# A convolution's layer norm emitted behind attention, with the out-projection in two halves

## The chip, the cores and the metric

The kernel runs on one core of one Trainium2 chip. The metric is the device time of one execution in microseconds (us); lower is better. TensorE is called PE here, VectorE DVE, ScalarE ACT, GpSimd POOL; SyncE's queue (SP) issues the DMAs.

## The reference, cut to what matters

Two transformer blocks follow each other on 512 tokens of width 1024. The change touches only the first one. It projects the normalised input, and out of the projection come two branches of 512 channels each: attention with 8 heads over 768 keys, and a convolution branch (a gated input, a depthwise convolution of width 31, a layer norm over the channels, swish, a pointwise product with w_pw). Both are gated, put side by side and multiplied with w_out:

```python
    y = jax.nn.silu(layer_norm(y, ln_w, ln_b))
    return y @ w_pw + b_pw
...
        attn = attend_blocked(q, k_all, v_all) * jax.nn.silu(p[..., ZA_LO:ZA_HI])
        conv = conformer_conv(...) * jax.nn.silu(p[..., ZC_LO:ZC_HI])
        out = jnp.concatenate([attn, conv], axis=-1) @ w_out[l]
        h = h + gate[:, None, :] * out
```

The second block (a recurrent mixer, a memory attention and a feed-forward part) takes h.

## The kernel before, in words

Channels lie on the 128 partitions and the 512 tokens along a row, so that 1024 channels are eight tiles of 128x512. Every large product is made of float32 values split into a high and a low part: `mm3` (line 181) issues three matmuls, high by high, high by low and low by high. A weight tile of 128x1024 is loaded into `wr`, copied by ACT into `wh` (the high part) and subtracted by DVE into `wl` (the rest); `Weights` (line 160) hands the tiles out in the order of its list and loads one ahead. There are two buffers of `wr` and `wl` and three of `wh`.

What is written in the source is an order of emission. A planner puts each engine's instructions into one fixed order by it: an instruction emitted earlier has priority, and one that could start sooner by the planner's own estimates may overtake it. On the chip each engine works through its order and waits where an operand is late. Two rules bind the planner further. The first writes of the buffers of one name come in the order in which the buffers were asked for (`wrote`, line 71). And `k.after` (line 84) puts an instruction behind another one that is named.

In the stretch of interest, from some 160 to 347 us, the first block does this:

- The convolution (`conv`, line 488) is 120 multiply-adds on DVE, written `hg<-hg,c` in the trace. They are emitted with a priority 1500 lower, so that they fill DVE's holes.
- Attention runs in eight half-steps, two for each pair of heads: `scores` (line 720) makes products into the PSUM tile `s` (two buffers of two banks), their maximum on DVE and the exponential into `p` on ACT; `values` (line 740) turns `p` around by PE transposes into `pt`, copies them by ACT into `xb`, and multiplies with the values into `pv`, in six chunks. The values of a half-step are emitted behind the scores of the next one. After both halves of a pair `att_out` (line 752) spreads the reciprocal sums through a buffer `tA` and four transposes, and multiplies; `att_split` (line 763) splits the result into `cat[0]` to `cat[3]`.
- `ln_pw` (line 662) is a generator that goes on by one step with each `next`: (1) the mean over channels by four matmuls with a constant matrix into `pj`, put behind the last matmul of attention emitted so far (`mark[0]`), and four subtractions; (2) four squares into `tA` and their sum; (3) the variance by small matmuls, a square root and a reciprocal; (4, 5) the reciprocal spread by transposes, and for each of four tiles the norm, the swish and the split, through `tA`; (6 to 9) the four pointwise products into `pj`, each with its gate and split into `cat[4]` to `cat[7]`. `LN_AFTER` (line 334) says behind which half-step each step is emitted: the mean behind the scores of half-step 4, steps 4 and 5 behind 5.5 and 6.5, the last three products behind 7.5.
- The out-projection (line 803) makes eight tiles of eight blocks each, the convolution's four blocks first, and takes a PSUM tile in turn from `pj`, `pt`, `pt` and `pv`. Each tile gets its gate and the input added (`xa`), is stored to `h1d`, and is split and squared for the next norm.

The first block has all eight PSUM banks: `pj` one, `s` two buffers of two, `pt` two, `pv` one.

Of the kernel before, what the change touches and what calls it, by code (L numbers as in the profile page):

```python
# [22 lines left out]
P = 128  # L23
S = 512
# [115 lines left out]
def split(k, src, hi, lo, dep=None):  # L140
    r = k.A.activation(hi, src, AF.Copy)
    if dep is not None:
        k.after(r, dep)
    rest(k, src, hi, lo)
# [15 lines left out]
class Weights:  # L160
# [14 lines left out]
    def next(self):  # L175
        i = self.i = getattr(self, "i", -1) + 1
        self.fill(i + 1 + self.ahead)
        return self.got[i]


def mm3(k, ps, wh, wl, ah, al, first, last):
    mm = k.T.matmul
    mm(ps, wh, ah, start=first, stop=False)
    mm(ps, wh, al, start=False, stop=False)
    k.mm = mm(ps, wl, ah, start=False, stop=last)
    return k.mm


def proj(k, ps, w, acts, order=None, tick=None):
    wh, wl = w  # L190
    order = list(order or range(len(acts)))
    for i, kt in enumerate(order):
        c = slice(kt * P, (kt + 1) * P)
        r = mm3(k, ps, wh[:, c], wl[:, c], acts[kt][0], acts[kt][1], i == 0, i == len(order) - 1)
        if tick:
            tick(r, 3)
# [67 lines left out]
def bcast(k, r, n, tag):  # L264
    b = k.t(tag)
    for j in range(n):
        k.T.transpose(b[:, j * P:(j + 1) * P], r[:, j:j + 1].to_broadcast([P, P]), k.ident)
    return b
# [62 lines left out]
    k.hka = small(k, k.vec("k_a", 0, 6), 6, 0.5)  # L331
    k.oka = small(k, k.vec("k_a", 0, 6), 6, -0.5, 1.0)

LN_AFTER = (4, 4.5, 5, 5.5, 6.5, 7, 7.5, 7.5, 7.5, 8)
MODW = 10
LATER = 1500
CTX = (0, 2)
# [3 lines left out]
def block1(k, I, st, h1d):  # L341
# [88 lines left out]
    ps = k.t("pj")  # L430
# [28 lines left out]
    for j in range(KT):  # L459
        raw, wh, wl = raws[j], k.t("wh", [1024], F32R), k.t("wl", [1024], F32R)  # L460
# [12 lines left out]
        for m in range(6):  # L473
            c = slice(m * P, (m + 1) * P)
# [13 lines left out]
    def conv(i):  # L488
# [3 lines left out]
        with k.tc.high_priority(offset=-LATER):  # L492
            for w in range(31):
                if w != 15:
# [2 lines left out]
                                           op0=ALU.mult, op1=ALU.add)  # L497

    W1 = Weights(k, [I["w_in"][0], I["w_in"][1]] + [I["w_q"][g] for g in range(4)] + [I["w_kv"][g] for g in range(2)]
                 + [I["w_in"][i] for i in (6, 7, 8, 9, 2, 3, 4, 5)] + [I["w_pw"][i] for i in range(2)] + [I["w_out"][i] for i in range(8)])  # L500
    W1.fill(1)
    for i in range(3):
        glu(accs[2 * i], accs[2 * i + 1])
# [13 lines left out]
    for g in range(4):  # L517
        wh, wl = W1.next()
        for kk in range(2):
            j = 2 * g + kk  # L520
            c = slice(kk * S, (kk + 1) * S)
            for t in range(4):
                tt = slice(t * P, (t + 1) * P)
                uh, ul = us[j]
                ps = q_ps[t // 2][:, t % 2, :]
# [18 lines left out]
    for t in (2, 3, 4, 5, 0, 1):  # L544
        ps = k.t("pt", [256])
        for j in range(KT):
            wh, wl = kw[j // 4]
            c = slice((j % 4) * 256, (j % 4 + 1) * 256)
            uh, ul = cus[j] if t < 2 else us[j]
            o = (t if t < 2 else t - 2) * P  # L550
# [76 lines left out]
    def zgates(n):  # L627
        for _ in range(min(n, 8 - len(gz))):
            i = len(gz)
            gz.append(zgate(zt[i] if i < 4 else "pj"))  # L630
# [19 lines left out]
    for g in range(2):  # L650
        for o, ts_ in ((0, range(2, 6)), (512, range(0, 2))):
            b = k.t("pt")
            n = len(ts_) * P
# [7 lines left out]
    cat = [None] * KT  # L661
    def ln_pw():
        mean = k.t("pj")
        for i in range(4):
            k.after(T.matmul(mean, k.ones512, ys[i], start=i == 0, stop=i == 3), mark[0])
        for i in range(4):
            V.tensor_tensor(out=ys[i], in0=ys[i], in1=mean, op=ALU.subtract)
        yield
        ss = SumSq(k, "tA")
        for i in range(4):  # L670
            ss.add(ys[i])
        yield
        r = ss.rstd("pj", k.inv512, 1e-6, k.cal([4]))
        yield
        rb = bcast(k, r, 4, "pj")
        ysl = []
        for i in range(4):
            V.tensor_tensor(out=ys[i], in0=ys[i], in1=rb, op=ALU.mult)
            t = k.t("tA")
            A.activation(t, ys[i], AF.Tanh, bias=k.hlb[:, i:i + 1], scale=k.hlw[:, i:i + 1])  # L680
            A.activation(ys[i], ys[i], AF.Identity, bias=k.vec("conv_ln_b", i), scale=k.vec("conv_ln_w", i))
            V.scalar_tensor_tensor(out=t, in0=t, scalar=1.0, in1=ys[i], op0=ALU.add, op1=ALU.mult)
            yh, yl = k.t("U", dt=F32R), k.t("U", dt=F32R)
            split(k, t, yh, yl)
            ysl.append((yh, yl))
            if i % 2:
                yield
        for m in range(4):
            if m % 2 == 0:
                wh, wl = W1.next()  # L690
            ps = k.t("pj")
            for j in range(4):
                c = slice((m % 2) * 512 + j * P, (m % 2) * 512 + (j + 1) * P)
                mm3(k, ps, wh[:, c], wl[:, c], ysl[j][0], ysl[j][1], j == 0, j == 3)
            t = k.t("tA")
            V.scalar_tensor_tensor(out=t, in0=ps, scalar=k.bpw2[:, m:m + 1], in1=gzc[m], op0=ALU.add, op1=ALU.mult)
            ch, cl = k.t("U", dt=F32R), k.t("U", dt=F32R)
            A.activation(ch, t, AF.Copy, scale=0.25)
            V.scalar_tensor_tensor(out=cl, in0=t, scalar=0.25, in1=ch.bitcast(F32), op0=ALU.mult, op1=ALU.subtract)
            cat[4 + m] = (ch, cl)  # L700
            k.dump("cat", 4 + m, ch.bitcast(F32))
            yield
# [4 lines left out]
    order = [2, 3, 4, 5, 0, 1]  # L707
    def heads(pr):
        qs = []
        for hh in range(2):  # L710
            h = 2 * pr + hh
            b = k.t("pt")
            for t in range(4):
                T.transpose(b[:, t * P:(t + 1) * P], flat(qr[t][pr // 2][:, h % 4]), k.ident)
            qhi, qlo = k.t("xa", dt=F32R), k.t("xa", dt=F32R)
            split(k, b, qhi, qlo)
            qs.append((qhi, qlo))
        return qs
# [21 lines left out]
    def values(pr, half, pts, pv):  # L740
        g = pr // 2
        for c in range(6):
            b = k.t("pt")
            for i in range(4):
                T.transpose(b[:, i * P:(i + 1) * P], pts[i][:, c * P:(c + 1) * P], k.ident)
            pT = k.t("xb")
            A.activation(pT, b, AF.Copy)
            for hh in range(2):
                mark[0] = T.matmul(pv[hh * 64:(hh + 1) * 64, half * 256:(half + 1) * 256], kvs[order[c]][:, 128 + g * 64:192 + g * 64],
                                   pT[:, hh * 256:(hh + 1) * 256], start=c == 0, stop=c == 5)  # L750
# [12 lines left out]
    def att_split(pr):  # L763
        ch, cl = k.t("U", dt=F32R), k.t("U", dt=F32R)
        split(k, gz[4 + pr], ch, cl)
        cat[pr] = (ch, cl)

    ln = ln_pw()
    zgates(ZG[1])
    qs = heads(0)  # L770
    zgates(ZG[2])
    pend, done = None, []
    for pr in range(4):
        for half in range(2):
            i = 2 * pr + half
            pts = scores(pr, half, qs)
            zgates(ZG[3 + i])
            for _ in range(LN_AFTER.count(i)):
                next(ln, None)
            if half == 1 and pr < 3:  # L780
                qs = heads(pr + 1)
            if len(gz) == 8:
                while done:
                    att_split(done.pop(0))
            if pend is not None:
                if pend[1] == 0:
                    pv = k.t("pv")
                values(*pend, pv)
                if pend[1] == 1:
                    att_out(pend[0], pv)  # L790
                    done.append(pend[0])
            for _ in range(LN_AFTER.count(i + 0.5)):
                next(ln, None)
            pend = (pr, half, pts)
    values(*pend, pv)
    att_out(3, pv)
    att_split(3)
    for _ in ln:
        pass

    S2.close()
    nm = Norm(k, "norm_mix_g", "hg", "xb")
    for m in range(KT):
        ps = k.t(("pj", "pt", "pt", "pv")[m % 4])
        proj(k, ps, W1.next(), cat, order=[4, 5, 6, 7, 0, 1, 2, 3])
        h = k.t("xa")
        Y.dma_start(out=h, in_=I["xT"][:, m, :])
        V.scalar_tensor_tensor(out=h, in0=ps, scalar=gate[:, m:m + 1], in1=h, op0=ALU.mult, op1=ALU.add)
        Y.dma_start(out=h1d[m], in_=h)
        k.dump("h1", m, h)  # L810
        nm.add(m, h)
# [677 lines left out]
def f32(a):  # L1489
    return np.ascontiguousarray(np.asarray(a), dtype=np.float32)  # L1490


def stat(w, cols):
    w = f32(w)
    kt = w.shape[0] // P
    return np.stack([w[:, c:c + P].reshape(kt, P, P).transpose(1, 0, 2).reshape(P, kt * P) for c in cols])
# [9 lines left out]
def pairs(w):  # L1506
    return np.ascontiguousarray(w.reshape(w.shape[0] // 2, 2, P, w.shape[2]).transpose(0, 2, 1, 3).reshape(w.shape[0] // 2, P, 2 * w.shape[2]))
# [7 lines left out]
def prepare(x, c, ctx, c_ctx, w_mod, b_mod, norm_w, w_in, q_norm_w, k_norm_w, conv_w, conv_b, conv_ln_w, conv_ln_b,  # L1515
# [3 lines left out]
    I = {}  # L1519
# [6 lines left out]
    w = f32(w_in[0])  # L1526
# [3 lines left out]
    I["w_q"] = mov(w[:, 0:512], 2)  # L1530
    I["w_kv"] = mov(w[:, 512:768], 4)
    I["w_pw"] = pairs(stat(w_pw[0], [128 * i for i in range(4)]))
    I["w_out"] = stat(w_out[0], [128 * i for i in range(8)])
    sw = np.concatenate([np.arange(16, 32), np.arange(0, 16), np.arange(48, 64), np.arange(32, 48)])
    qn, kn = f32(q_norm_w[0]), f32(k_norm_w[0])
    I["rows"] = f32(np.stack([qn, qn[sw], kn, kn[sw], f32(mem_q_norm_g_2[0]), f32(mem_k_norm_g_2[0])]))
# [46 lines left out]
```

## Time and profile before

| | us |
|---|---|
| median of 3 runs | 1144.32 |
| lowest and highest | 1142.23, 1146.53 |
| the profiled execution | 1144.24 |
| its span, first to last instruction | 1142.5 |
| PE busy in the span | 1084.6 (95%) |
| DVE, ACT busy | 726.8, 537.5 |
| PE's mean granted clock, as a share of 2.4 GHz | 0.979 |

The span is the time that the rows count from. A row of a timeline gives its start, its duration, the engine, the instruction with what it writes and reads, how many such instructions are merged in it, and in brackets how long the engine was idle before it and who released it. PE's rows overlap at their ends, since matmuls are pipelined; the distance from start to start is what one costs in a stream. All instructions pass through a helper and bear the same line number, L57, so they are told apart by their tiles.

### The profile page before, as it was taken

To read this page: it belongs to the slowest core of one execution; us is meant where nothing else is said; L and a number is where in the kernel's file an instruction comes from. 1 tells how busy PE (TensorE), PEld (TensorE's weight loads), DVE (VectorE), ACT (ScalarE), POOL (GpSimd) and SP (SyncE) were. 2 spreads that over 40 slices of the span, in tenths; PEclk is the share of its full clock that TensorE was granted. 3 is DMA by queue.
4 is the path that set the end of the run, shared out by engine and by line. 5 is a ranking of instruction groups with operands and counts; after the bars stand their busy time and mean duration, and the time that the engine had idled before them with its cause. 6 is when DMAs were issued, how large, how long until landed. Compare 5 with 4: busy or idle time off the path is not lost.

```text
span 1142.5 us, 15940 instructions
## 1 busy us (share of the span) xinstructions
PE 1084.6 (95%) x6272; PEld 836.6 (73%) x6272; DVE 726.8 (64%) x1253; ACT 537.5 (47%) x987; POOL 67.6 (6%) x223
## 2 busy tenths in 40 slices
PE   8989989985998899999999898999999999999998
PEld 3768966553787677777777676768888888888887
DVE  3469999986354688888876888657444334334332
ACT  5344546767335366464645565555434134233220
POOL 0000000000001112111111112010000000000000
PEclk8999999997999999999989998999999999999999
DMA  9653221000243111010101221212222333233232
GB/s 337 258 182 105 73 76 38 1 30 26 71 151 118 55 46 49 20 38 20 38 20 52 74 75 38 74 56 93 92 93 93 95 107 93 92 95 107 93 116 88
DMA packets 32203, 96.46 MB, mean 84 GB/s; under 512 B 3456, under 2 KB 6272, under 8 KB 32128
## 3 DMA queue, kind: packets, MB, share of 16 engines
q1 hardware_dynamic: 32128, 95.45, 25.3%
q8 instruction: 49, 0.80, 0.3%
q14 instruction: 26, 0.21, 0.1%
HBM read 91.24 MB, written 4.19 MB: 84 GB/s over the span
## 4 chain that ended last, share of the span: by engine, by line
PE 83%; DVE 5%; ACT 4%; POOL 3%; DMA 2%; issue 2%; SPq 0%; ACTq 0%; POOLq 0%; DVEq 0%
PE pf L57 31%; PE pj L57 23%; PE pt L57 7%; PE i L57 7%; PE s L57 7%; PE pv L57 5%; PE y L57 3%; POOL nr L57 3%; DVE hg L57 1%; ACT p L57 1%; ACT tA L57 1%; DVE c L57 1%; ACT wh L57 1%; DMA x<-xT 1%; DMA wr<-rw_in 1%
## 5 line engine op out<-in xcount | busy, mean ns | idle before, releaser
L57 ACT ACTIVATE wh<-wr 128x1024 fp32r<-128x1024 f32 (+1 forms) x132 | 137.6, 1043 | 186.7 <-PE pf L57 74.6
L57 DVE TENSOR_TENSOR wl<-wr,wh 128x1024 fp32r<-128x1024 f32 (+1 forms) x132 | 158.7, 1203 | 20.3 <-PE pt L57 12.6
L57 PE MATMUL pf<-A,wh 128*128 128x512 f32 x512 | 157.8, 390 | 0.0
L57 PE MATMUL pj<-hg,wh 128*128 128x512 f32 x448 | 153.6, 415 | 2.5 <-ACT r L57 1.1
L57 ACT ACTIVATE f<-i 128x512 f16<-128x512 f32 (+1 forms) x132 | 71.9, 598 | 91.5 <-PE i L57 91.4
L57 PEld LDWEIGHTS pf<-A,wh 128*128 128x128 f32 x512 | 96.0, 188 | 19.8
L57 PE MATMUL pf<-A,wl 128*128 128x512 f32 x256 | 99.7, 389 | 0.0
L57 PEld LDWEIGHTS pj<-hg,wh 128*128 128x128 f32 x448 | 80.7, 191 | 19.6 <-issue 2.0
L57 DVE TENSOR_TENSOR x<-x,pf 128x512 f32<-128x512 f32 (+1 forms) x33 | 22.2, 672 | 113.9 <-PE pf L57 113.9
L57 PE MATMUL pj<-hg,wl 128*128 128x512 f32 x224 | 90.4, 404 | 1.5 <-DVE wl L57 1.5
L57 DVE SCALAR_TENSOR_TENSOR hg<-hg,c 128x499 f32<-128x499 f32 (+14 forms) x120 | 85.0, 739 | 0.8 <-ACT hg L57 0.4
L57 PE MATMUL pf<-ff,wh 128*128 128x512 f32 (+1 forms) x272 | 79.7, 377 | 0.0
L57 PE MATMUL pf<-hg,wh 128*128 128x512 f32 x256 | 78.8, 389 | 0.0
L57 DVE SCALAR_TENSOR_TENSOR fr<-pf,r 128x512 f32<-128x512 f32 x32 | 22.1, 691 | 85.4 <-PE pf L57 82.1
L57 ACT ACTIVATE fr<-fr 128x512 f32<-128x512 f32 x32 | 20.2, 632 | 99.9 <-DVE fr L57 99.9
L57 PEld LDWEIGHTS <-f 128*128 128x128 f16 x720 | 45.8, 100 | 23.0 <-issue 13.3
L57 PE MATMUL i<-f 128*128 128x128 f16 x672 | 55.6, 225 | 5.4 <-DVE f L57 5.3
L57 PE MATMUL pj<-U,wh 128*128 128x512 f32 x160 | 54.2, 416 | 3.4 <-DVE hg L57 3.0
L57 PEld LDWEIGHTS pf<-ff,wh 128*128 128x128 f32 x272 | 50.1, 188 | 9.5
L57 PEld LDWEIGHTS pf<-A,wl 128*128 128x128 f32 x256 | 48.1, 188 | 10.0
L57 PEld LDWEIGHTS pf<-hg,wh 128*128 128x128 f32 x256 | 48.1, 188 | 10.0
L57 PE MATMUL pf<-ff,wl 128*128 128x512 f32 (+1 forms) x136 | 51.2, 377 | 0.0
(305 smaller groups left out, 2125.8 us busy)
## 6 DMA issues: line engine op xcount, KB each, us to landing
wr<-w_ff SPq DMA_DIRECT2D x64, 512.0 KB, 3.5
modw<-w_mod SPq DMA_DIRECT2D x20, 512.0 KB, 7.2
wr<-rw_in SPq DMA_DIRECT2D x20, 512.0 KB, 3.5
wr<-w_out SPq DMA_DIRECT2D x16, 512.0 KB, 3.5
wr<-w_in SPq DMA_DIRECT2D x10, 512.0 KB, 3.6
wr<-w_start SPq DMA_DIRECT2D x8, 384.0 KB, 5.8
x<-xT SPq DMA_DIRECT2D x8, 256.0 KB, 6.1
modw<-w_mod SPq DMA_DIRECT2D x8, 256.0 KB, 6.2
```

Source lines behind the costliest of these rows:

```text
L57: r = f(*a, **kw)
```

## The change

`LN_AFTER` goes, and with it the steps of `ln_pw` between the half-steps. When all of attention is emitted, five steps of `ln_pw` follow (up to the norm's split), then the out-projection's attention half for the tiles 0 to 5, then the pointwise products, then the attention half of the tiles 6 and 7, then the convolution's half of all eight tiles. The eight sums stay open in the eight PSUM banks meanwhile: four in the two `s` buffers, two in `pt`, one each in `pj` and `pv`. The tiles 0 to 3 take the first three blocks of attention first and the fourth behind them. The pointwise products take `pj` and `pv` in turn. The weights of the out-projection are stored in two halves, two tiles to a load; there are as many loads of the same size as before, in another order.

```diff
--- before.py
+++ after.py
@@ -331,7 +331,6 @@
     k.hka = small(k, k.vec("k_a", 0, 6), 6, 0.5)
     k.oka = small(k, k.vec("k_a", 0, 6), 6, -0.5, 1.0)
 
-LN_AFTER = (4, 4.5, 5, 5.5, 6.5, 7, 7.5, 7.5, 7.5, 8)
 MODW = 10
 LATER = 1500
 CTX = (0, 2)
@@ -497,7 +496,8 @@
                                            op0=ALU.mult, op1=ALU.add)
 
     W1 = Weights(k, [I["w_in"][0], I["w_in"][1]] + [I["w_q"][g] for g in range(4)] + [I["w_kv"][g] for g in range(2)]
-                 + [I["w_in"][i] for i in (6, 7, 8, 9, 2, 3, 4, 5)] + [I["w_pw"][i] for i in range(2)] + [I["w_out"][i] for i in range(8)])
+                 + [I["w_in"][i] for i in (6, 7, 8, 9, 2, 3, 4, 5)] + [I["w_outa"][i] for i in range(3)]
+                 + [I["w_pw"][i] for i in range(2)] + [I["w_outa"][3]] + [I["w_outb"][i] for i in range(4)])
     W1.fill(1)
     for i in range(3):
         glu(accs[2 * i], accs[2 * i + 1])
@@ -688,7 +688,7 @@
         for m in range(4):
             if m % 2 == 0:
                 wh, wl = W1.next()
-            ps = k.t("pj")
+            ps = k.t(("pj", "pv")[m % 2])
             for j in range(4):
                 c = slice((m % 2) * 512 + j * P, (m % 2) * 512 + (j + 1) * P)
                 mm3(k, ps, wh[:, c], wl[:, c], ysl[j][0], ysl[j][1], j == 0, j == 3)
@@ -775,8 +775,6 @@
             i = 2 * pr + half
             pts = scores(pr, half, qs)
             zgates(ZG[3 + i])
-            for _ in range(LN_AFTER.count(i)):
-                next(ln, None)
             if half == 1 and pr < 3:
                 qs = heads(pr + 1)
             if len(gz) == 8:
@@ -789,20 +787,47 @@
                 if pend[1] == 1:
                     att_out(pend[0], pv)
                     done.append(pend[0])
-            for _ in range(LN_AFTER.count(i + 0.5)):
-                next(ln, None)
             pend = (pr, half, pts)
+    oacc = []
+
+    def outa(m, w, kts):
+        wh, wl = w
+        for kt in kts:
+            c = slice(m % 2 * 512 + kt * P, m % 2 * 512 + (kt + 1) * P)
+            mm3(k, oacc[m], wh[:, c], wl[:, c], cat[kt][0], cat[kt][1], kt == 0, False)
+
     values(*pend, pv)
     att_out(3, pv)
     att_split(3)
+    for _ in range(5):
+        next(ln)
+    w01 = [W1.next(), W1.next()]
+    for i in range(2):
+        a = k.t("s", [2, S])
+        oacc += [a[:, 0, :], a[:, 1, :]]
+    for kts in ((0, 1, 2), (3,)):
+        for m in range(4):
+            outa(m, w01[m // 2], kts)
+    w = W1.next()
+    for m in (4, 5):
+        oacc.append(k.t("pt"))
+        outa(m, w, range(4))
     for _ in ln:
         pass
+    w = W1.next()
+    for m in (6, 7):
+        oacc.append(k.t(("pj", "pv")[m % 2]))
+        outa(m, w, range(4))
 
     S2.close()
     nm = Norm(k, "norm_mix_g", "hg", "xb")
     for m in range(KT):
-        ps = k.t(("pj", "pt", "pt", "pv")[m % 4])
-        proj(k, ps, W1.next(), cat, order=[4, 5, 6, 7, 0, 1, 2, 3])
+        if m % 2 == 0:
+            wh, wl = W1.next()
+        ps = oacc[m]
+        for kt in range(4):
+            c = slice(m % 2 * 512 + kt * P, m % 2 * 512 + (kt + 1) * P)
+            mm3(k, ps, wh[:, c], wl[:, c], cat[4 + kt][0], cat[4 + kt][1], False, kt == 3)
         h = k.t("xa")
         Y.dma_start(out=h, in_=I["xT"][:, m, :])
         V.scalar_tensor_tensor(out=h, in0=ps, scalar=gate[:, m:m + 1], in1=h, op0=ALU.mult, op1=ALU.add)
@@ -1530,7 +1555,8 @@
     I["w_q"] = mov(w[:, 0:512], 2)
     I["w_kv"] = mov(w[:, 512:768], 4)
     I["w_pw"] = pairs(stat(w_pw[0], [128 * i for i in range(4)]))
-    I["w_out"] = stat(w_out[0], [128 * i for i in range(8)])
+    for n, o in (("w_outa", 0), ("w_outb", 512)):
+        I[n] = pairs(stat(f32(w_out[0])[o:o + 512], [128 * i for i in range(8)]))
     sw = np.concatenate([np.arange(16, 32), np.arange(0, 16), np.arange(48, 64), np.arange(32, 48)])
     qn, kn = f32(q_norm_w[0]), f32(k_norm_w[0])
     I["rows"] = f32(np.stack([qn, qn[sw], kn, kn[sw], f32(mem_q_norm_g_2[0]), f32(mem_k_norm_g_2[0])]))
```

## Rows read from the trace of the kernel before

**Rows 1.** Windows, by stage: length, busy us of each engine, PEclk, DMA share, GB/s.

```profile
160.00:254.20 94.20, 87.40 (x529) 59.69 (x528) 85.68 (x146) 61.92 (x120) 0.00 (x0) 1.00 0.07 23
254.20:274.70 20.50, 7.51 (x31) 5.35 (x30) 14.25 (x27) 13.80 (x22) 0.00 (x0) 0.72 0.17 52
274.70:304.30 29.60, 29.15 (x155) 18.20 (x154) 13.63 (x20) 15.86 (x27) 0.00 (x0) 0.96 0.12 36
304.30:347.00 42.70, 42.70 (x190) 35.31 (x188) 22.66 (x30) 16.07 (x22) 0.00 (x0) 1.00 0.38 130
```

**Rows 2.** Windows of 2 us, one inside the gap, same columns.

```profile
264.00:266.00 2.00, 1.19 (x6) 1.19 (x6) 0.81 (x2) 1.70 (x3) 0.00 (x0) 0.50 0.01 4
```

**Rows 3.** Timeline of PE, 254 to 277: start, us, instruction, idle before and releaser.

```profile
254.20 0.74 PE L57 MATMUL s<-kst,xa 128*128 128x512 f32 x3
255.89 0.97 PE L57 MATMUL s<-kst,xa 128*128 128x512 f32 x4 [0.95 <-ACT p L57]
257.88 0.98 PE L57 MATMUL s<-kst,xa 128*128 128x512 f32 x4 [1.02 <-ACT p L57]
258.92 1.12 PE L57 MATMUL pj<-hg,c 128*128 128x512 f32 x2
264.81 1.86 PE L57 MATMUL pj<-g,tA 128*128 128x1 f32 x8 [4.77 <-DVE tA L57]
267.25 1.11 PE L57 MATMUL pj<-g,c 128*128 128x128 f32 x4 [0.57 <-DVE c L57]
273.98 1.11 PE L57 MATMUL pt<-g,tA 128*128 128x128 f32 x4 [5.62 <-ACT tA L57]
274.74 1.28 PE L57 MATMUL pj<-U,wh 128*128 128x512 f32 x2
```

**Rows 4.** Timeline of ACT and DVE in the same stretch.

```profile
273.31 0.61 ACT L57 ACTIVATE tA<-c 128x512 f32<-128x512 f32 x1
258.14 0.72 DVE L57 SCALAR_TENSOR_TENSOR hg<-hg,c 128x497 f32<-128x497 f32 x1
279.48 0.69 DVE L57 TENSOR_TENSOR U<-tA,U 128x512 fp32r<-128x512 f32 x1 [0.22 <-ACT U L57]
```

**Rows 5.** Timeline of PE, one stretch of attention values and of the first mean.

```profile
212.28 1.18 PE L57 MATMUL pv<-xb,kvs 128*64 128x256 f32 x8
213.39 1.10 PE L57 MATMUL pt<-g,p 128*128 128x128 f32 x8
214.25 0.94 PE L57 MATMUL s<-kst,xa 128*128 128x512 f32 x4
223.62 2.74 PE L57 MATMUL pj<-hg,c 128*128 128x512 f32 x6
```

**Rows 6.** Timeline of PE at the next block's start.

```profile
341.32 0.62 PE L57 MATMUL pv<-U,wh 128*128 128x512 f32 x2
346.76 0.61 PE L57 MATMUL pj<-hg,wh 128*128 128x512 f32 x2
348.90 0.50 PE L57 MATMUL pj<-hg,wl 128*128 128x512 f32 x1 [1.52 <-DVE wl L57]
354.06 0.95 PE L57 MATMUL pj<-g,xb 128*128 128x1 f32 x8
355.57 0.65 PE L57 MATMUL pj<-g 128*128 128x128 f32 x4 [0.57 <-DVE g L57]
```

**Rows 7.** Timeline of ACT and DVE, the first out-projection weights.

```profile
289.93 1.06 ACT L57 ACTIVATE wh<-wr 128x1024 fp32r<-128x1024 f32 x1 [2.24 <-PE pj L57]
290.84 1.22 DVE L57 TENSOR_TENSOR wl<-wr,wh 128x1024 fp32r<-128x1024 f32 x1
```

**Rows 8.** Timeline of PE at its lower clock.

```profile
157.08 1.03 PE L57 MATMUL pj<-U,wh 128*128 128x512 f32 x2 [2.50 <-DVE hg L57]
158.33 1.05 PE L57 MATMUL pj<-U,wh 128*128 128x512 f32 x2
```

**Rows 9.** SyncE's queue, the load of the seventh tile's input.

```profile
311.75 0.33 SPq L57 DMA_DIRECT2D xa<-xT  x1
```

## The prediction

> **What bounds the kernel now.** I read the stages first. Over the span PE is busy 95%, so only a stage in which PE waits can give much back. From 160 to 254 us PE is busy 87.4 of 94.2 us and DVE 85.7: attention and convolution together keep both near full. From 304 to 347 us, the out-projection, PE is busy all of 42.7 us. Between them PE does 7.5 us of work in 20.5 us, at a mean clock of 0.72 [rows 1], and inside it the clock stands at 0.50, the lower level of 1.2 GHz [rows 2].
>
> PE's timeline says what these 20 us are. After the last scores and the mean it waits 4.77 us for DVE's sum of squares, 0.57 for the reciprocal, and 5.62 for ACT's buffer `tA` [rows 3]. The last wait matters most. What PE waits for is `att_out` of the third pair, four transposes that need no more than attention's sums. Their input is written at 273.31, after the norm's tanh [rows 4], because both use `tA` and the norm asked for it first. The values of the last two half-steps ask for `pt` behind those transposes, so twelve chunks of ready attention work stand behind the layer norm. The norm in turn waits for the convolution, whose last multiply-add starts at 258.14 [rows 4]. So the stage is bound by one chain, convolution, norm, swish, during which PE has work that it may not touch.
>
> **The work of the stretch.** I take it from the start of the last scores, 254.20 [rows 3], to the first matmul of the next block, 346.76 [rows 6]: 92.6 us. PE's work in it, at full clock:
> - scores: 0.74 + 0.97 + 0.98 = 2.7 us [rows 3].
> - values, twelve chunks: two chunks take 1.97 us from start to start (212.28 to 214.25 [rows 5]), so six times that, 11.8 us.
> - two `att_out`: four transposes cost 0.65 at full clock in the next block's norm [rows 6], so 1.3 us.
> - the mean: eight records; six took 2.74 [rows 5], so 3.7 us. Before, only two of the eight stood inside the stretch (1.12 us [rows 3]), so 2.6 us of them are new there.
> - variance and spread, 0.95 + 0.65 = 1.6 us [rows 6].
> - pointwise product and out-projection: 48 + 192 matmuls. A tile of 24 takes 5.44 us (341.32 to 346.76 [rows 6]), 0.227 each, together 54.4 us. Halving the out-projection's tiles leaves the count of matmuls as it is.
>
> Sum 75.5 us. The slack of before is 17.1 us: waits 0.95 + 1.02 + 4.77 + 0.57 + 5.62 = 12.9 [rows 3]; the lower clock, 0.9 for the variance, 0.5 for each of two groups of transposes (against [rows 6]) and about 1 for the first pointwise matmuls, 2.9; and 1.3 left over at changes between kinds of matmuls, which I keep.
>
> **What the change removes and adds.**
> - *Order of buffers.* Attention asks for `tA` and `pt` ahead of the norm now. The values of half-step 6 can follow those of 5 at 254 us, beside the scores. This takes away the 5.62 us wait. What is late next is the exponential of the last scores: PE idles 7% from 160 to 254 [rows 1], and 7% of the 17 us of attention work left is 1.2 us. Bounds 0 (tiles of the out-projection fill it) and 3.
> - *An added wait.* The mean stands behind the last values matmul, hence near 272 instead of 259, and ends near 275. Behind it in PE's order stand up to six half tiles, 6 x 2.72 = 16.3 us, which need only `cat[0]` to `cat[3]`. From the mean's end to the first pointwise matmul took 14.7 us (260.04 to 274.74 [rows 3]), to the fourth split pair 20.1 (280.17 [rows 4]). With the variance and the spread at full clock that is 18.7. Cover: 16.3 + 1.6, and the first pointwise tile's three blocks 2.0, 19.9 in all. So the chain is just hidden. But tiles that the planner sets ahead of the mean don't cover it. I expect some 3 us ahead, hence 2.0 us of idleness. Bounds: 0 with none ahead; 7 with the first 36 matmuls (8.2 us) ahead.
> - *Weights.* The third load's split waits until the first weights are free, after tile 1's fourth block. ACT and DVE need 2.1 us (289.93 to 292.06 [rows 7]) against 1.36 us of matmuls of tiles 2 and 3. Its `wl` stands in DVE's queue among the norm's steps, and they behind it. I take 0.5 us, bounds 0 and 2.5. The later loads have 5.4 us of matmuls each, as before.
> - *The second half's cover.* `cat[4]` to `cat[7]` have the attention half of tiles 6 and 7 over them, 5.4 us; gate and split take some 2.1 (three steps of about 0.7, as [rows 4]). Nothing, up to 1 if buffers of `U` come late.
> - *The tail.* A tile leaves every 2.72 us instead of 5.44. DVE was busy 22.7 us for about eight tiles [rows 1], 2.8 each, so it is level with PE at the end. The next block already waited 1.52 us for DVE's `wl` [rows 6]. I take 0, bounds -1.5 and +1.5. SP issues as many loads and stores as before, in half the time; the stage moved 130 GB/s, and the second half would move about double in its 22 us. The seventh input is asked for when the first tile has left, at 311.75, 7.5 us into the stage [rows 1, 9]; that would do in the second half too, where it is needed after 16 us. PE waits for no evacuation, since all eight sums have their own bank.
>
> Left idle: 1.3 + 1.2 + 2.0 + 0.5 = 5.0. Gain 17.1 - 5.0 = 12.1 us. The profiled execution took 1144.24 us, 0.08 below the median of 1144.32, so both give 1132.
>
> **The rivals.**
> - *All covered* (0.11). No idleness beyond the 1.3 us, and the next block loses its 1.52 us wait: 17.1 - 1.3 + 1.5 = 17.3 us, 1127. For it: 19.9 us of cover against 18.7. Against: PE's fixed order, in which any misjudged step costs.
> - *Half covered* (0.12). The first 36 matmuls stand ahead of the mean: 7.0 us idle under the chain, about 3 us of lower clock as before, and 1 us for the weights. Gain 17.1 - 1.3 - 11.0 = 4.8, 1139.5. For it: the four `s` sums come free with the last exponentials, well before the mean.
> - *Slower: the chain stands bare at another place* (0.06). All six half tiles run ahead of the mean. Then 18.7 - 1.6 - 2.0 = 15.1 us idle and 2.9 of lower clock stand against a slack of 17.1 - 1.3 = 15.8: 2.2 us lost, with the weights' 0.8 and the tail's 1.5 some 4.5, 1149. It decides from about 13 us of tiles ahead of the mean on. Against it: filling needs holes in PE, and attention's tail has only a few us of them.
> - *Clock* (0.03). Moving from sum to sum in six banks with short waits keeps PE at 1.2 GHz through the attention half. Three matmuls took 1.25 us there (157.08 to 158.33 [rows 8]) instead of 0.68: 24 x 0.57 = 13.7 us, 1146. The Trainium skill, "TensorE: Matmul & The Clock Gate", section "A second HAM failure mode: psum-queue depth-cycling", tells of a kernel that lost its full clock again and again in the small waits while it cycled through PSUM banks. By that rule the forecast would fall to this rival; the trace speaks against it, since before the out-projection changed banks every 24 matmuls at clock 1.00 [rows 1].
> - *Nothing moves* (0.04). Another shared buffer ties attention's tail to the norm as `tA` did: 1144. I found none: `s`, `p`, `xb` and `pv` are asked for by attention first.
>
> **How the numbers follow.** The forecast has 0.64. A measurement of this kernel can tell about 0.5%, 5.7 us. Forecast, the first rival and half of the second lie beyond it: 0.81 faster. The other half, clock, nothing-moves and the milder part of the slower rival: 0.13 the same. Slower by more: 0.06. The range holds the forecast with its bounds, most of the first rival and of the second: 1126.5 to 1139.5.
>
> **What would show it.** Right: transposes of `p` follow at 254 without the 5.62 us wait; the mean comes near 272 with eight records in a row; `pt<-U` matmuls stand between it and the pointwise ones; PEclk 1.00 throughout; the next block starts near 334.5. Wrong: waits of PE for `tA` or `c` over 4 us in all after the mean, a clock of 0.50 there, tiles of the out-projection ahead of the mean by more than 8 us, or a longer wait for `wl` at the next block's start.

## The result, and the profile after

The changed kernel took 1128.38 us (median of 4 runs, 1126.26 to 1130.51) against 1143.74 for the kernel before, run beside it (4 runs, 1142.23 to 1146.53). The ratio is 0.9875 with a 95% interval of 0.9851 to 0.9898: 14.3 us less, between 11.7 and 17.0. The two medians lie 15.4 us apart; the 14.3 is worked out from the ratio. The forecast was 1132.0 and a gain of 12.1.

The profiled execution took 1126.26 us (span 1124.5) against 1144.24 (span 1142.5). Of these 18.0 us, 3.5 are not the change's: both programs give PE the same instructions up to 223 us, yet the first pair's `att_out` already stands at 205.64 before

```profile
205.64 0.60 PE L57 MATMUL pt<-g,tA 128*128 128x128 f32 x4
```

and at 202.16 after:

```profile
202.16 0.60 PE L57 MATMUL pt<-g,tA 128*128 128x128 f32 x4
```

Runs of one and the same program differ nearly as much: three of the kernel called "first weights" below have it at 202.47, 205.80 and 204.35. The granted clock of the first 40 us is 0.87 before and 1.00 after, but that is not all of it, since the three have 1.00, 0.91 and 1.00 there. From here on I measure from that `att_out`, which takes the difference out.

The profile's first part after the change, PE's line: busy time, share of the span, instructions.

```profile
PE 1076.2 (96%) x6272; PEld 832.4 (74%) x6272; DVE 726.4 (65%) x1253; ACT 537.6 (48%) x987; POOL 67.5 (6%) x223
```

The changed kernel by stage, the columns as in [rows 1]. The stages are bounded by the second and third pair's `att_out`, the mean, the first pointwise matmul, the end of the out-projection, and the next block's first matmul on `lw`.

```profile
223.68:246.40 22.72, 20.92 (x143) 14.14 (x142) 20.76 (x36) 16.64 (x32) 0.00 (x0) 1.00 0.07 24
246.40:266.33 19.93, 19.12 (x133) 12.51 (x132) 10.78 (x20) 12.04 (x23) 0.00 (x0) 1.00 0.17 54
266.33:286.80 20.47, 19.53 (x85) 14.48 (x84) 14.41 (x22) 12.75 (x18) 0.00 (x0) 1.00 0.17 51
286.80:326.17 39.37, 38.90 (x169) 31.00 (x167) 27.02 (x36) 18.47 (x27) 0.00 (x0) 1.00 0.41 134
326.17:359.04 32.87, 27.66 (x117) 22.25 (x117) 14.80 (x20) 15.35 (x21) 5.66 (x11) 0.90 0.37 118
```

The stage that was 37% busy at a clock of 0.72 [rows 1] is gone. From 246.40 to 326.17 PE does nothing for 0.81 + 0.94 + 0.47 = 2.2 us, at a clock of 1.00 throughout. The last line is the exception, at 0.90 with 5.2 us in which PE is idle; the same stretch before is shorter, at 1.00 with 3.2 us idle:

```profile
346.92:374.75 27.83, 24.63 (x117) 20.03 (x116) 13.31 (x18) 12.64 (x17) 5.18 (x11) 1.00 0.40 130
```

PE's timeline after the change (start, us, instruction, idle before and releaser), against [rows 3]:

```profile
246.40 0.60 PE L57 MATMUL pt<-g,tA 128*128 128x128 f32 x4
...
256.03 0.71 PE L57 MATMUL s<-U,wh 128*128 128x512 f32 x2
...
264.77 1.14 PE L57 MATMUL pv<-xb,kvs 128*64 128x256 f32 x8
...
266.33 3.60 PE L57 MATMUL pj<-hg,c 128*128 128x512 f32 x8
...
274.81 0.95 PE L57 MATMUL pj<-g,tA 128*128 128x1 f32 x8
...
277.78 0.60 PE L57 MATMUL pj<-g,c 128*128 128x128 f32 x4
...
282.09 0.50 PE L57 MATMUL pt<-U,wl 128*128 128x512 f32 x1 [0.94 <-DVE wl L57]
...
286.80 0.61 PE L57 MATMUL pj<-U,wh 128*128 128x512 f32 x2
...
293.06 0.74 PE L57 MATMUL pj<-U,wh 128*128 128x512 f32 x2 [0.47 <-DVE tA L57]
```

The third `att_out` comes without a wait. Nine matmuls of the out-projection (`s<-U`, from 256.03) fill holes of attention's tail; then the mean stands as eight records in a row. Half tiles lie around the variance (274.81) and the spread (277.78), so neither shows the waits of 4.77 and 0.57 that it had. The view of PE's waits from 246 to 327 (us in total, times, longest) is all that is left:

```profile
PE pt L57 <- DVE wl L57: 0.9, 1, 0.9
PE pv L57 <- ACT xb L57: 0.7, 2, 0.3
PE pj L57 <- DVE tA L57: 0.5, 1, 0.5
```

So against before, in the profiled pair: 2.6 us less up to the second `att_out` (24.08 to 21.52 from the first one), 14.7 less from there to the end of the out-projection, 5.0 more at the next block's start (27.83 to 32.87), and 2.3 less in the 765 us behind it. Together 14.5. The last term can't be put down to the change: among all kernels below, whose program is the same there, this distance went from 763.8 to 768.7 us.

### The profile page after: what moved, and what is told of

Its sections match the earlier page's. It is cut to its first block, busy times and chain, and to the rows that moved or that the text cites. A ratio compares the mean times of both kernels' runs of the same rounds, so it can differ in the third digit from the quotient of the medians.

```text
span 1124.5 us, 15949 instructions
## 1 busy us (share of the span) xinstructions
PE 1076.2 (96%) x6272; PEld 832.4 (74%) x6272; DVE 726.4 (65%) x1253; ACT 537.6 (48%) x987; POOL 67.5 (6%) x223
## 4 chain that ended last, share of the span: by engine, by line
PE 83%; DVE 5%; ACT 4%; POOL 3%; DMA 3%; issue 2%; SPq 0%; ACTq 0%; DVEq 0%; POOLq 0%
PE pf L57 31%; PE pj L57 22%; PE s L57 9%; PE i L57 7%; PE pt L57 6%; PE pv L57 5%; PE y L57 3%; POOL nr L57 3%; DMA modw<-w_mod 1%; ACT p L57 1%; DMA wr<-w_start 1%; DVE wl L57 1%; DVE hg L57 1%; ACT wh L57 1%; ACT xb L57 1%
## 5 line engine op out<-in xcount | busy, mean ns | idle before, releaser
L57 PEld LDWEIGHTS <-f 128*128 128x128 f16 x720 | 46.0, 100 | 23.7 <-issue 14.7
L57 PEld LDWEIGHTS pj<-hg,wl 128*128 128x128 f32 x224 | 42.9, 192 | 9.8 <-DVE wl L57 1.3
```

The lines of the kernel that those rows point to most:

```text
L57: r = f(*a, **kw)
```

## The experiments

"Stretch" is from the first `att_out` to the end of the out-projection, "entry" from there to the first matmul on `lw`, both of the profiled execution; the median is of all runs of a kernel. Each ratio is against runs of the kernel before made beside it, whose median went from 1142.50 to 1143.82, so differences to the first line's median do not give it.

| kernel | stretch, us | entry, us | median, us | ratio (95%) |
|---|---|---|---|---|
| before | 141.28 | 27.83 | 1143.74 | |
| changed | 124.01 | 32.87 | 1128.38 | 0.9875 (0.9851 to 0.9898) |
| own buffer | 136.87 | 30.21 | 1141.06 | 0.9983 (0.9959 to 1.0006) |
| whole tiles | 140.08 | 28.13 | 1142.48 | 1.0011 (0.9985 to 1.0038) |
| old place | 138.07 | 31.19 | 1143.10 | 0.9990 (0.9967 to 1.0013) |
| two tiles | 134.35 | 33.10 | 1139.60 | 0.9976 (0.9952 to 1.0000) |
| four tiles | 129.63 | 31.91 | 1134.61 | 0.9930 (0.9903 to 0.9957) |
| block order | 124.65 | 30.50 | 1128.58 | 0.9871 (0.9849 to 0.9894) |
| first weights | 124.03 | 29.89 | 1127.37 | 0.9862 (0.9833 to 0.9891) |
| first weights in before | 141.24 | 28.02 | 1143.53 | 1.0006 (0.9981 to 1.0030) |
| changed, again | 124.07 | 33.11 | 1128.84 | 0.9877 (0.9847 to 0.9907) |
| first weights, again | 124.08 | 26.93 | 1124.18 | 0.9844 (0.9816 to 0.9872) |
| changed, third | 124.01 | 31.34 | 1128.94 | 0.9862 (0.9838 to 0.9886) |
| first weights, third | 124.00 | 27.20 | 1127.01 | 0.9852 (0.9827 to 0.9877) |

### Own buffer: the tie through `tA` cut, nothing else

```diff
 (before)
-    k.open(S2, "att", dict(q2=8, p=8))
+    k.open(S2, "att", dict(q2=8, p=8, rx=1))
...
-        rx = k.t("tA", [8, 64])
+        rx = k.t("rx", [8, 64])
```

> The kernel before with one edit: the spread sums of att_out get a buffer of their own (rx) instead of one of the norm's tA. Theory 'tie' (the gap is attention standing behind the norm through tA): the values of the last two half-steps move into the gap, the 5.62 us wait of the transposes goes, and the norm's chain (14.7 us to the first pointwise matmul, 20 to the fourth pair) runs beside 15.8 us of attention work; some 5 to 8 us of idleness stay. 1144 - 10 = 1134 us, between 1131 and 1137. Theory 'cover' (only the six half tiles of the out-projection can fill the chain): attention alone changes little, 1140 to 1144 us.

The stretch became 4.4 us shorter. The median is 1.4 us below the 1142.50 of the kernel before beside it, and the ratio's interval holds 1: the tie by itself is not the 12 us. PE's timeline of this kernel:

```profile
276.65 0.50 PE L57 MATMUL pj<-U,wh 128*128 128x512 f32 x1 [4.27 <-ACT U L57]
...
282.92 0.50 PE L57 MATMUL pj<-U,wh 128*128 128x512 f32 x1 [0.96 <-DVE U L57]
...
284.58 0.73 PE L57 MATMUL pj<-U,wh 128*128 128x512 f32 x2 [0.93 <-DVE tA L57]
...
288.44 0.74 PE L57 MATMUL pj<-U,wh 128*128 128x512 f32 x2 [0.84 <-DVE tA L57]
...
292.35 0.74 PE L57 MATMUL pj<-U,wh 128*128 128x512 f32 x2 [0.39 <-DVE tA L57]
...
296.25 0.74 PE L57 MATMUL pj<-U,wh 128*128 128x512 f32 x2 [0.84 <-DVE tA L57]
```

The 5.62 us wait is gone, and the freed values now run under the variance's wait of 4.77. But they are used up before the swish, on which PE waits 4.27; and where they had stood between the pointwise products, those now wait for their one sum's bank to be read out, 0.93 + 0.84 + 0.39 + 0.84 = 3.0 us. These waits, with one of 0.23 behind the first, are 8.5 us, and five of 0.23 to 0.31 for `xb` are 1.4 more; they stand in place of the 12.9 [rows 3]. Over the stretch PE's idle time falls from 17.2 to 13.5 us and its busy time, at a clock of 0.99 instead of 0.95, from 124.1 to 123.3, which makes the 4.4. The ready work that the tie held back had been covering something later.

### Whole tiles: the norm behind attention, nothing to cover it

```diff
 (changed)
-    for _ in range(5):
-        next(ln)
...
     for _ in ln:
         pass
...
-        ps = oacc[m]
...
+        ps = k.t(("pj", "pt", "pt", "pv")[m % 4])
+        proj(k, ps, W1.next(), cat, order=[4, 5, 6, 7, 0, 1, 2, 3])
```

The out-projection and its loads are whole again, as before; the pointwise products still take `pj` and `pv` in turn.

> The changed kernel without its halves: the whole norm and the pointwise product behind attention, then the out-projection whole in eight tiles of 24 matmuls. Theory 'cover': attention is untied but the chain lies bare, some 15 us of idleness and 3 us of lower clock more than in the changed kernel: 1128.4 + 17 = 1145 us, 1142 to 1148. Theory 'tie': untying is what pays, 1131 to 1137 us.

The same time as before, the stretch 1.2 us shorter. PE's timeline has the whole chain bare, 4.76 + 0.57 + 6.33 us, and the doubled 1.86, 1.11 and 1.52 us of the lower clock behind each wait:

```profile
275.02 1.86 PE L57 MATMUL pj<-g,tA 128*128 128x1 f32 x8 [4.76 <-DVE tA L57]
277.45 1.11 PE L57 MATMUL pj<-g,c 128*128 128x128 f32 x4 [0.57 <-DVE c L57]
284.89 1.52 PE L57 MATMUL pj<-U,wh 128*128 128x512 f32 x2 [6.33 <-ACT U L57]
```

### Old place: the half tiles, with the norm's steps inside attention

```diff
 (changed)
+LN_AFTER = (4, 4.5, 5, 5.5, 6.5)
...
+            for _ in range(LN_AFTER.count(i)):
+                next(ln)
...
-    for _ in range(5):
-        next(ln)
```

> The changed kernel with the norm's first five steps emitted between the half-steps again, at the old places 4, 4.5, 5, 5.5 and 6.5; the halves of the out-projection stay, six half tiles ahead of the pointwise product. Theory 'tie': att_out of the third pair stands behind the norm's tA again, so the gap of 259 to 274 us comes back and the six tiles, which need attention, come too late to fill it: 1140 to 1145 us. Theory 'cover': the six tiles are there to fill the chain wherever it stands: 1127 to 1132 us.

The stretch is 3.2 us shorter, and the entry 3.4 us longer. The half tiles that PE can reach take the place of the norm's early waits (4.77 and 0.57 are gone, 2.64 for `p` stands there), but the others come behind `att_out` of the third pair, which has its wait for `tA` back to the hundredth, 5.62 us, with the lower clock's 1.12 behind it.

```profile
262.77 0.73 PE L57 MATMUL s<-U,wh 128*128 128x512 f32 x2 [2.64 <-ACT p L57]
...
271.36 1.12 PE L57 MATMUL pt<-g,tA 128*128 128x128 f32 x4 [5.62 <-ACT tA L57]
```

So untying alone gives 4.4 us of the stretch, the late norm without cover 1.2, cover without untying 3.2; the change, which has all, 17.3.

### Two tiles and four tiles: the dose

```diff
 (changed)
-    for m in (4, 5):
...
     for _ in ln:
         pass
+    for m in (4, 5):
...
```

The diff is that of the four tiles, without the order of the loads, which follows it; the two-tile kernel moves half tiles 2 and 3 behind as well.

> The changed kernel with two half tiles instead of six ahead of the pointwise product (5.4 us of cover instead of 16.3); the half tiles 2 to 7 follow behind it. Theory 'cover': 10.9 us less cover, of which 1 to 2 us were not needed, and about 2 us of lower clock: 1128.4 + 11 = 1139 us, 1136 to 1142. Theory 'tie': the cover hardly matters, 1128 to 1132 us.

> The changed kernel with four half tiles instead of six ahead of the pointwise product. From att_out of the first pair to the end of the out-projection the runs so far took 140.1 us with the whole out-projection behind (no cover), 134.4 with two half tiles and 124.0 with six. Theory 'cover' (each half tile of 2.72 us laid under the norm's chain takes its own time off, until the chain is covered): 128 to 129.5 us for this stretch, and 1132 to 1136 us in all. Rival 'threshold' (only a full cover keeps the clock up, less is worth little): 132 to 134 us for the stretch and 1137 to 1141 us.

The stretch is 140.08, 134.35, 129.63 and 124.01 us with none (whole tiles), two, four and six half tiles ahead: 5.7, 4.7 and 5.6 us for each two, whose own 24 matmuls take 5.44 [rows 6]. Each half tile takes about its own time off, and there is no threshold in the stretch; the 129.63 lies just outside the 128 to 129.5 expected. In the whole time two tiles show only 2.9 us of it, since their entry is 5 us longer than that of whole tiles. PE's longest wait in each kernel shows what is still bare, the one ahead of the first pointwise matmul. With two tiles:

```profile
286.30 1.52 PE L57 MATMUL pj<-U,wh 128*128 128x512 f32 x2 [6.33 <-ACT U L57]
```

and with four:

```profile
288.31 1.52 PE L57 MATMUL pj<-U,wh 128*128 128x512 f32 x2 [5.01 <-ACT U L57]
```

With six it has none (286.80, above).

### Block order: the fourth block not held back

```diff
 (changed)
-    for kts in ((0, 1, 2), (3,)):
+    for kts in ((0, 1, 2, 3),):
```

> The changed kernel with the half tiles 0 to 3 taking their four blocks of attention at once, tile by tile, instead of three blocks of all four tiles first and the fourth behind. The fourth block needs cat[3], split some 3.5 us after the last values matmul, which is when the mean's 3.6 us end. Theory 'split late': the mean covers that split, so 0 to 1 us are lost: 1128 to 1129.5 us. Rival 'stall': tile 0 waits for cat[3] and the planner, which knows of it, has less to put into attention's last holes: 2 to 3 us lost, 1130 to 1132 us.

The stretch is 0.6 us longer, the time the same within its interval. `cat[3]` comes last out of attention, but the mean's 3.60 us stand ahead of its blocks, and PE's timeline has no wait there; the order by blocks is worth nothing measurable here.

### First weights: the next block's first load split earlier

```diff
 (changed)
-                 + [I["w_pw"][i] for i in range(2)] + [I["w_outa"][3]] + [I["w_outb"][i] for i in range(4)])
+                 + [I["w_pw"][i] for i in range(2)] + [I["w_outa"][3]] + [I["w_outb"][i] for i in range(4)] + [I["rw_in"][18]])
...
+    k.w18 = W1.got[-1]
...
-    wa = slab(k, 18, W.next(), hg, norm_rows, "wa")
+    W.marks.append(k.mm)
+    W.fill(1)
+    wa = slab(k, 18, k.w18, hg, norm_rows, "wa")
```

This asks where the 5 us at the entry come from. In the changed kernel PE's timeline there reads:

```profile
327.98 0.73 PE L57 MATMUL pj<-hg,wh 128*128 128x512 f32 x2 [1.81 <-ACT wh L57]
329.59 0.50 PE L57 MATMUL pj<-hg,wl 128*128 128x512 f32 x1 [0.88 <-DVE wl L57]
...
337.50 0.94 PE L57 MATMUL pj<-g 128*128 128x128 f32 x4 [1.83 <-DVE g L57]
339.12 1.22 PE L57 MATMUL pj<-hg,wh 128*128 128x512 f32 x2 [0.69 <-ACT r L57]
```

DVE's timeline shows the split of the first weights, behind the eighth tile's gate (326.21):

```profile
326.21 0.75 DVE L57 SCALAR_TENSOR_TENSOR xa<-pv,c,xa 128x512 f32<-128x512 f32 x1 [0.50 <-PE pv L57]
...
328.23 1.30 DVE L57 TENSOR_TENSOR wl<-wr,wh 128x1024 fp32r<-128x1024 f32 x1
```

SyncE's queue holds the next load until that split has read its buffer, which is at 329.53:

```profile
329.56 7.71 SPq L57 DMA_DIRECT2D wr<-rw_in  x3
```

and ACT has that load's split ahead of the table and the square root:

```profile
334.60 1.06 ACT L57 ACTIVATE wh<-wr 128x1024 fp32r<-128x1024 f32 x1 [3.79 <-DMA wr<-rw_in]
335.68 1.28 ACT L57 ACT_TABLE_LOAD   x1
336.97 0.26 ACT L57 ACTIVATE g<-pj,g 128x4 f32<-128x4 f32 x1
```

> The changed kernel with the next block's first weight tile (rw_in 18) asked for inside the out-projection, ahead of tile 6, instead of behind all eight tiles. In the changed kernel the way from the last out-projection matmul to the first matmul on lw is 32.9 us, before 27.8. Theory 'entry' (the faster second half leaves ACT and DVE no hole for these weights: their split comes behind the eighth tile's evacuation, 1.81 and 0.88 us of waiting, and holds the next load back, on which ACT then waits ahead of the square root, and the clock falls): the waits for wh and wl go, the way is 28 to 29 us, and 2 to 4 us of the time go, 1124 to 1126.5 us. Rival 'hidden' (the next block's own chain swallows what is won at its entry): the entry is shorter, the time the same as the changed kernel's, 1127 to 1130 us.

> The kernel before with the same edit: rw_in 18 asked for ahead of the last of its eight tiles. Theory 'entry': the slow second half had holes for these weights, so only the 1.52 us wait for wl can go: 1141 to 1142.5 us, against 1142.5 before. Rival: the weights cost as much here, 3 us or more.

In the changed kernel the waits of 1.81 and 0.88 become one of 0.59, that for the spread falls from 1.83 to 1.26, and the entry from 32.87 to 29.89, where 28 to 29 was expected:

```profile
327.08 0.70 PE L57 MATMUL pj<-hg,wh 128*128 128x512 f32 x2 [0.59 <-DVE xa L57]
...
334.84 0.65 PE L57 MATMUL pj<-g 128*128 128x128 f32 x4 [1.26 <-DVE g L57]
336.18 1.22 PE L57 MATMUL pj<-hg,wh 128*128 128x512 f32 x2 [0.69 <-ACT r L57]
```

In the kernel before, the same edit takes away the `wl` wait of 1.52 [rows 6], but with 1.63 for the spread instead of 0.57 and 0.69 for `r` instead of 1.11: PE is idle for 2.3 us instead of 3.2. The entry stays at 28.02 all the same, since its 117 matmuls were busy for 25.70 us there, at a clock of 0.94, instead of 24.63. The time did not fall either, where 1141 to 1142.5 was expected.

The loss at the entry thus has two parts. PE's idle time in it is 3.2 us before, 5.2 in the changed kernel and 2.5 with the first weights earlier. This part is one of order on ACT and DVE, and the edit takes it back. The waits of 1.81 and 0.88 stand in every kernel with halved tiles that leaves the weights where they were (old place, two and four tiles and block order too), and the 1.52 alone in own buffer and whole tiles: they come with the halves. Before, ACT split these weights from 343.45 on, 3.5 us ahead of the out-projection's end; in the changed kernel it does so at 326.89, 0.7 us behind it. The busy time of the same 117 matmuls is 24.63, 27.66 and 27.35 us, at clocks of 1.00, 0.90 and 0.89. So of the 5.0 us lost, 2.0 are idle time and 3.0 the lower clock, which this edit left as it was in its first run.

The 0.9862 of this kernel is not apart from the changed kernel's 0.9875, its median lies in the range of the rival "hidden", and its six runs fall into 1123.5 to 1124.2, at a mean granted clock of 0.988, and 1130.5 to 1131.9, at 0.980 to 0.981. So both were run again, twice, side by side.

> The changed kernel once more, beside the next run on the same chip. Its four runs so far took 1126.3 to 1130.5 us. Both theories: a median of 1128 to 1130 us, and in its trace again about 124.0 us from att_out of the first pair to the out-projection's end.

> The changed kernel with the next block's first weights asked for ahead of tile 6, once more, to be set against the changed kernel on the same chip. Theory 'entry': the 3.0 us that its trace won at the next block's entry last to the end: 2 to 3 us below the changed kernel, 1125 to 1127 us. Rival 'hidden': within 1 us of it, since later waits and the clock in the next block take them back.

> The changed kernel once more, as the companion of the next run. Both theories: 1127 to 1130 us.

> The changed kernel with the next block's first weights asked for ahead of tile 6, a third time. So far its runs lie near 1124 or near 1131, and its two traces differ at the next block's entry by 3 us, with a mean clock there of 0.89 in the one and 1.00 in the other. Theory 'entry': a mean over all runs of 2 to 4 us below the changed kernel's. Rival 'hidden': within 1 us.

Side by side the medians were 1128.84 and 1124.18, then 1128.94 and 1127.01. Over all runs the changed kernel has a mean of 1128.57 (13 runs, standard deviation 1.49), the first-weights one 1126.47 (16 runs, 3.11): 2.1 us less, with a standard error of 0.88 and so between 0.3 and 3.9. It is the best version found, by little. The entry's waits are nearly the same in its runs, but not its clock. By windows, first run and second:

```profile
326.50:356.39 29.89, 27.35 (x117) 22.42 (x117) 13.73 (x20) 13.79 (x19) 4.65 (x11) 0.89 0.37 116
```

```profile
329.88:356.81 26.93, 24.54 (x117) 20.37 (x117) 13.74 (x20) 13.80 (x19) 4.65 (x11) 1.00 0.42 128
```

Behind the wait for `r`, of 0.69 us in both, the first two matmuls took 1.22 us in the first run (above) and 0.73 in the second:

```profile
339.41 0.73 PE L57 MATMUL pj<-hg,wh 128*128 128x512 f32 x2 [0.69 <-ACT r L57]
```

## Why the prediction was right, and which terms were not

**The cause held, as two parts that need each other.** That `att_out` stands behind the norm through `tA` is shown by own buffer, where the wait goes with the shared buffer, and by old place, where it returns at the same 5.62 us. That cover is the other part is shown by the dose and by whole tiles. The forecast counted both in one sum and did not say that either by itself would be nearly nothing in the time (own buffer 0.9983, old place 0.9990, whole tiles 1.0011). A third thing, the pointwise sums in turn in `pj` and `pv`, was taken out of no kernel: own buffer, which has them all in `pj`, waits 3.0 us for that bank where the changed kernel waits 0.47, but what this is worth by itself is not shown.

**The mean** came at 266.33, 269.8 with the 3.5 us of the earlier start added back, where 272 was forecast. The 2.6 us that its first six records no longer take inside attention are enough for the rest. 2.0 us of tiles stood ahead of it, where some 3 were expected.

**The term "2.6 us of them are new there" was mis-sized.** It charged the stretch for six records of the mean and gave attention no credit for losing them, though 2.74 stood in [rows 5]. First to second `att_out` fell by 2.56. With the credit the sum would have been 14.7. The 1.3 "left over" has the same charge in it: without the 2.6, the stretch of before leaves 3.9.

**The idleness left was mis-sized:** 2.2 us by the windows where the sum kept 5.0. The kinds of change and the attention tail (1.3 + 1.2) kept some 0.8 (0.35 + 0.31 for `xb`, the rest between records), the weights 0.94 instead of 0.5, and of the 2.0 us under the chain (18.7 less 16.9 of cover would be 1.8) nothing is left; the last 0.47 is PE waiting until the first pointwise sum is read out of `pj`, where the prediction had put waits for evacuation at nothing. The chain itself was not shorter: from the mean's end at 269.93 to the fourth split pair, which ends at 291.16, it took 21.2 us instead of 18.7. Of these 2.5 us, 1.5 lie between the reciprocal's end on DVE, 276.27, and the spread at 277.78, which stands behind half tiles in PE's order. Two splits of weights stand in the chain's way as well, the third load's on ACT ahead of the norm's second table load, and a later one on ACT and DVE ahead of the fourth pair:

```profile
276.09 0.18 DVE L57 RECIPROCAL c<-c 128x4 f32<-128x4 f32 x1 [1.45 <-ACT c L57]
...
289.34 1.23 DVE L57 TENSOR_TENSOR wl<-wr,wh 128x1024 fp32r<-128x1024 f32 x1 [0.26 <-ACT wh L57]
290.48 0.68 DVE L57 TENSOR_TENSOR U<-tA,U 128x512 fp32r<-128x512 f32 x1
```

```profile
278.66 1.06 ACT L57 ACTIVATE wh<-wr 128x1024 fp32r<-128x1024 f32 x1 [2.60 <-PE s L57]
279.74 1.28 ACT L57 ACT_TABLE_LOAD   x1
```

What covered it beyond the forecast's 19.9 us was the second pointwise tile: with its sum in `pv`, its first three blocks run (from 289.00) ahead of most of the first tile's fourth. The two mis-sized terms come to 2.6 + 2.8 = 5.4 us, and the stretch did 5.2 us better than 12.1 (17.3 in all).

**The tail's "I take 0, bounds -1.5 and +1.5" was wrong, beyond its bounds.** The entry lost 5.0 us in the profiled run and 5.3 and 3.5 in the two repeats: 2.0, 2.3 and 1.9 of it idle time, beyond the bound by itself, and the rest a lower clock (0.90, 0.90 and 0.95), of which the term says nothing. The step had seen that DVE is level with PE at the end and that PE had waited 1.52 for `wl`; it did not follow what stands behind that split: the buffer it holds, the load that waits for the buffer, and ACT's split of that load ahead of the square root. PE waits 2.69 us for the first weights instead of 1.52, and once more at the spread, 1.83 instead of 0.57; at `r` it gets 0.4 back. One of the prediction's signs of being wrong, "a longer wait for `wl` at the next block's start", came in substance: `wl` itself shows 0.88, but behind 1.81 for `wh` of the same split. What lowered the clock there is not shown. This error went against the two others, so the total came out nearer (14.3 measured, 12.1 forecast) than its parts deserve. The next block started at 327.98, 331.5 with the 3.5 us, where 334.5 was forecast.

**The rivals.** "All covered" came closest in the stretch, 2.2 us of idleness, but it also wanted the entry's 1.52 us back, where more was lost; the gain lies between its 17.3 and the forecast's 12.1. "Half covered" and "the chain stands bare" needed 8 to 13 us of tiles ahead of the mean; there were 2.0. "Nothing moves" fell with the 5.62. The clock rival fell with the windows: 1.00 over 80 us, in which up to eight sums lie open in their banks at once and PE goes from one to another every 1 to 12 matmuls. The rule that stood beside it (the Trainium skill, "TensorE: Matmul & The Clock Gate", section "A second HAM failure mode: psum-queue depth-cycling") is about a kernel whose PE idled briefly between its groups of matmuls; here PE's waits come to 2.1 us in all, and changing banks alone did not lower the clock.

## What to carry to other kernels

When ready work stands behind a chain only because two steps share a buffer's name, cutting the tie moves the work but doesn't shorten the chain: look for what the held-back work was covering later, and bring as many microseconds of independent matmuls as the chain has, in the order in which PE will stand there. A term for work moved into a stretch has its twin, with the other sign, in the stretch that it left. And where a stage gets denser, follow the first load of the next stage through all in-order queues (split, buffer, next load, next split), since a hole that the change fills may be where that split used to run.

## What was not expected of the hardware

The same program with nearly the same waits ran its entry at a granted clock of 0.89 in one run and 1.00 in another, 29.89 against 26.93 us. What decides it is not shown: at the entry the waits ahead of the fall were 0.59, 1.26 and 0.69 us, and where the clock stayed up 0.59, 1.12 and 0.69 in the second run and 0.59, 1.38 and 0.69 in the third, so the longer wait alone does not. The first 40 us, in programs alike up to there, ran at clocks from 0.87 to 1.00; the first `att_out` came between 202.13 and 205.80 us, and at a clock of 1.00 alone between 202.13 and 204.35.
